# One written order for the RWKV part: the steps of three pairs of heads and of the output projection alternate on TensorE

## The chip, the cores and the metric

The program runs on one core of a Trainium2 chip. What counts is the device time of one execution in microseconds (us). Engines: PE is TensorE (matmuls; PEld is its weight load), DVE is VectorE, ACT is ScalarE, POOL is GpSimd, and SP is SyncE, which issues the DMAs here. Each engine works through its own instructions in the order in which they were emitted, and waits at an instruction until the semaphores it needs have come.

## The reference, cut to what matters

Two transformer blocks run one after the other on 512 tokens of width 1024. The change lies in the second block, in the RWKV mixer (six heads of 64) and in the output projection:

```
w = -softplus(-(w0 + tanh(wd) @ w2)) - 0.5;  a = sigmoid(a0 + ad @ a2);  g = sigmoid(gd) @ g2
kk = k*k_k / max(norm(k*k_k), eps);  k = k*(1 + (a-1)*k_a)
for each token t:  S = S*exp(-exp(w)) + (S @ -kk) (kk*a)^T + v k^T;   y[t] = S r
y = (groupnorm(y)*ln_w + ln_b + sum(r*k*r_k)*v) * g
x = x + concat(attention, y, memory attention) @ w_out
x = x + conv_ffn(rms_norm(x))
```

## The kernel before

Large products are split products: a weight tile is split into a rounded part `wh` (ACT) and a rest `wl` (DVE), and `mm3` issues three matmuls of 128x512, which appear in the profile at lines 161, 163 and 165. A program planner (the tile scheduler) sets the order of the instructions on each engine; what is written first has priority, and a stretch can be given a lower priority.

The token loop is computed in chunks of 64 tokens. The six heads are three pairs (0, 1, 2), one 128-partition tile for each pair; the index `e` is the head in the pair. For a pair there are four parts. `prep` makes decays, normalised keys and transposed copies. `grams` makes the products within the chunks (`NM`) and the first `X` and `XT`. Five levels invert a triangular matrix by doubling: `level` computes per head T = mask*(NM X) (line 1430, evicted by DVE at 1431), then the new X (1435, ACT copy 1437) and the new XT (1440, DVE copy 1442), eight 64x64 matmuls each. `finish` makes `G` (1449), the products `pzx`, `pq`, `py`, a chain of six steps over the chunks (`S`, 1482 and 1483), the group norm, and the split result `obh[i]`, `obl[i]`.

PSUM has eight banks here: two `mm`, two `aux`, three `rw` (levels) and one `wo`.

`w_out_attention`, called W below, is the projection of the five tiles that attention gives: eight blocks (one for each output tile `hl[m]`), each with its own 320 KB load into `wr`, split into `wh` and `wl` (one buffer each), 15 matmuls into the bank `wo`, and an add into `hl[m]` on DVE. It is written with the priority lowered by 3000, and so its blocks fill what the RWKV part leaves. The projection of the RWKV tiles (`w_out`, `w_out_add`) comes last: 512 KB loads straight into three `NM` buffers, tiles 0 and 1 in one accumulation, tile 2 in a second, through the two `mm` banks. The feed-forward part follows.

The parts are called in this order: W (low priority), grams 0, five levels of pair 0, prep 1, grams 1, finish 0, prep 2, levels of pair 1, grams 2, finish 1, levels of pair 2, finish 2, projection. Only the planner mixes them.

Of the kernel before, what the change touches and what calls it, by code (L numbers as in the profile page):

```python
# [10 lines left out]
F32R = mybir.dt.float32r  # L11
# [46 lines left out]
def _build(ctx, tc, ins, out, stop, dbg):  # L58
# [96 lines left out]
    def mm3(pieces, w, xs, first, last, mcol):  # L155

        whi, wlo = w
        xhi, xlo = xs
        c = slice(mcol, mcol + 128)
        for p, s in pieces:  # L160
            pe.matmul(p, whi[:, c], xhi[:, s], start=first, stop=False)  # L161
        for p, s in pieces:
            pe.matmul(p, whi[:, c], xlo[:, s], start=False, stop=False)  # L163
        for p, s in pieces:
            pe.matmul(p, wlo[:, c], xhi[:, s], start=False, stop=last)  # L165
# [669 lines left out]
    RW, WPRI = 3, -3000  # L835
# [361 lines left out]
    def prep(i):  # L1197

        o = B()
        mm = "mm" if i else "aux"  # L1200

# [14 lines left out]
        pe.matmul(pa, lw[32:64, ic], lora[32:64], start=True, stop=True, tile_position=(32, 0))  # L1216
# [3 lines left out]
        dve.tensor_tensor_scan(out=L, data0=reset, data1=sw, initial=0.0, op0=ALU.mult, op1=ALU.add)  # L1220
        pool.tensor_tensor(out=sw, in0=L, in1=sw, op=ALU.subtract)
# [6 lines left out]
        q = work()  # L1228
        act.activation(out=q, in_=k, func=AF.Square, scale=V("k_k", i))
        pc = ps(8, tag="aux")  # L1230
        for b in range(4):
            pe.matmul(pc[:, 2 * b : 2 * b + 2], q[:, b * 128 : (b + 1) * 128], blk2, start=True, stop=True)
        rn = tm(8, "rn", 2)
        act.activation(out=rn, in_=pc, func=AF.Sqrt)
        dve.tensor_scalar(out=rn, in0=rn, scalar1=L2_EPS, scalar2=None, op0=ALU.max)
        dve.reciprocal(out=rn, in_=rn)
        x = q
        dve.tensor_copy(out=x.rearrange("p (c d) -> p c d", d=64), in_=rn.unsqueeze(2).to_broadcast([128, 8, 64]))
        pb = ps(512, tag="aux")
        for b in range(4):  # L1240
            pe.transpose(pb[:, b * 128 : (b + 1) * 128], x[:, b * 128 : (b + 1) * 128], ident)
        kkn = q
        dve.scalar_tensor_tensor(out=kkn, in0=pb, scalar=V("k_k", i), in1=k, op0=ALU.mult, op1=ALU.mult)
# [10 lines left out]
        dve.scalar_tensor_tensor(out=a, in0=a, scalar=V("r_k", i), in1=r, op0=ALU.mult, op1=ALU.mult)  # L1254
        pb = ps(512, tag=mm)
        pe.matmul(pb, blk1, a, start=True, stop=True)
        o.bonus = tp(512, "bonus", "q")
        dve.tensor_tensor(out=o.bonus, in0=pb, in1=v, op=ALU.mult)
        o.RH = RH = tp(1024, "RH").rearrange("p (t e c) -> p t e c", t=4, e=2)
        o.BT, o.KT, o.VT = [tp(512, n, "q") for n in ("BT", "KT", "VT")]  # L1260
        for n, (src, dst) in enumerate(((AR, None), (bt, o.BT), (kt, o.KT), (v, o.VT))):
            pt = ps(512, tag="aux")
            for b in range(4):
                pe.transpose(pt[:, b * 128 : (b + 1) * 128], src[:, b, 0] if dst is None else src[:, b * 128 : (b + 1) * 128], ident)
            if dst is None:
                act.copy(out=RH[:, :, :, 0:64], in_=pt.rearrange("p (t e c) -> p t e c", t=4, e=2))
            else:
                act.copy(out=dst, in_=pt)
        return o

    cur.bufs = {"u": 4, "cv": 4}
    with sub("e_x", "xp"), sub("e_w", "wp"), sub("e_t", "sm"):
# [34 lines left out]
        for n, (name, i) in enumerate(order):  # L1307
# [12 lines left out]
            if name in ("l", "r", "k", "v"):  # L1320
                shifted(u, {"r": 0, "k": 3, "v": 6, "l": 9}[name] + i, lora if name == "l" else rkv[name][i])
                if n == PREPN:
# [3 lines left out]
                    first_prep = prep(0)  # L1326
# [40 lines left out]
    st = [first_prep, None, None]  # L1367
# [22 lines left out]
    def grams(i, o):  # L1390
        o.NM, o.X, o.XT = [], [], []
        for e in range(2):
            hr = hs[e]
            nm = nmt()
            NM = nm.rearrange("p (b m c) -> p b m c", b=4, m=4)
            for b in range(4):
                if b % 2 == 0:
                    p2 = ps(512)
                p = p2[:, b % 2 * 256 : b % 2 * 256 + 256]
                for x, s in ((o.kt, 0), (o.bt, 128)):  # L1400
                    for q in range(2):
# [12 lines left out]
            pt = rw()[:, 0:256]
            for b, r, c in bq:
                pe.matmul(pt[r, c], XT[r, c], ident[r, r], start=True, stop=True)
            act.copy(out=X, in_=pt)
            act.copy(out=o.RH[:, :, e, 64:128], in_=c4(pk))
            o.NM.append(NM)
            o.X.append(X)  # L1420
            o.XT.append(XT)

    def level(o, l):

        for e in range(2):
            X, XT, NM = o.X[e], o.XT[e], o.NM[e]
            T = wk(256, f"T{e}", 2)
            p = rw()[:, 0:256]
            for b, r, c in bq:
                pe.matmul(p[r, c], NM[r, b, 2], X[r, c], start=True, stop=True)  # L1430
            dve.tensor_tensor(out=c4(T), in0=c4(p), in1=lev[l].unsqueeze(1).to_broadcast([128, 4, 64]), op=ALU.mult)
            if l < 4:
                p = rw()[:, 0:256]
                for b, r, c in bq:
                    pe.matmul(p[r, c], XT[r, c], T[r, c], start=True, stop=True)  # L1435
                o.X[e] = wk(256, f"X{e}", 2)
                act.copy(out=o.X[e], in_=p)
            p = rw()[:, 0:256]
            for b, r, c in bq:
                pe.matmul(p[r, c], T[r, c], XT[r, c], start=True, stop=True)  # L1440
            o.XT[e] = wk(256, f"XT{e}", 3)
            dve.tensor_copy(out=o.XT[e], in_=p)

    def finish(i, o):
        G = []
        for e in range(2):
            p = rw()
            for b, r, c in bq:
                pe.matmul(p[r, b * 128 : (b + 1) * 128], o.XT[e][r, c], o.RH[r, b, e], start=True, stop=True)
            g = wk(512, f"G{e}", 1)  # L1450
            act.mul(out=g, in_=p, mul=-1.0)
            G.append(v4(g))
        half = lambda x, q: x.rearrange("p (b q c) -> p b q c", b=4, q=2)[:, :, q]
        pq, pzx = [rw()[:, 0:256] for _ in range(2)], [ps(512), ps(512)]
        for n, (b, r, c) in enumerate(bq):
            for e in range(2):
                pe.matmul(pq[n % 2][hs[e], c], G[e][r, b, 0:64], o.NM[e][r, b, 3], start=True, stop=True)
        for e in range(2):
            hr = hs[e]
            for n in range(8):  # L1460
# [9 lines left out]
        AT = ftmp()  # L1470
        for q in range(2):
            dve.tensor_tensor(out=half(AT, q), in0=pzx[q][:, 0:256].rearrange("p (b c) -> p b c", b=4), in1=eye64.unsqueeze(1).to_broadcast([128, 4, 64]), op=ALU.add)
        lend = o.lend
        S = ftmp()
        XS = ftmp()
        for q in range(2):
            dve.tensor_tensor(out=half(XS, q), in0=pzx[q][:, 256:512].rearrange("p (b c) -> p b c", b=4), in1=lend[:, q::2].unsqueeze(2).to_broadcast([128, 4, 64]), op=ALU.mult)
        act.copy(out=S[:, 64:128], in_=XS[:, 0:64])
        for n in range(1, 7):
            p = ps(64, tag="aux")  # L1480
            for e in range(2):
                pe.matmul(p[hs[e]], AT[hs[e], n * 64 : n * 64 + 64], S[hs[e], n * 64 : n * 64 + 64], start=True, stop=True)
            dve.scalar_tensor_tensor(out=S[:, n * 64 + 64 : n * 64 + 128], in0=p, scalar=lend[:, n : n + 1], in1=XS[:, n * 64 : n * 64 + 64], op0=ALU.mult, op1=ALU.add)
        py = [ps(256) for _ in range(2)]
        for n, (b, r, c) in enumerate(bq):
            for e in range(2):
                pe.matmul(py[n % 2][hs[e], c], G[e][r, b, 64:128], o.NM[e][r, b, 3], start=True, stop=False)
            for e in range(2):
                pe.matmul(py[n % 2][hs[e], c], o.VT[r, b * 128 + 64 * e : b * 128 + 64 * e + 64], o.NM[e][r, b, 1], start=False, stop=True)
        y = ftmp()  # L1490
# [223 lines left out]
```

## Time and profile before

| | us |
|---|---|
| median of 3 runs | 2334.19 (2330.99 to 2338.97) |
| profiled execution, its own time | 2327.18 |
| its span | 2325.4 |
| PE busy in the span | 2230.1 (96%) |
| DVE busy | 1622.7 (70%) |
| ACT busy | 935.1 (40%) |
| mean granted TensorE clock | 0.982 |
| share of PE in the chain that ended last | 87% |

The stretch that the change rewrites begins at 1757 us of the span, when the last attention of the second block is done, and ends at 1948 us, when the last `hl` has been added; the feed-forward part takes the rest. In the windows the clock is a share of full speed: 1.00 is 2.4 GHz, 0.50 is 1.2 GHz. PE's busy time is modelled, and a group of small matmuls that run side by side is best timed from start to start.

### The profile page before, as it was taken

The page shows a single profiled execution, that of the slowest core. Times are in us where ns is not written, and L with a number is a line of the kernel's source. Part 1 is how long each engine was busy: PE and PEld are TensorE (multiplying, and loading weights), DVE is VectorE, ACT ScalarE, POOL GpSimd, SP SyncE. Part 2 cuts the span into 40 slices and gives each one's busy share as a digit, 9 for nine tenths or more (in the row PEclk, how much of TensorE's full clock was granted, in tenths as well). Part 3 has the DMA queues.
Part 4 walks back from the last instruction along what each step waited for, and adds up shares of the span by engine and source line. Part 5 has one row for each costly group of instructions (what it writes and reads, how often), then busy time and mean ns, then how long its engine had stood idle before and what let it go on. Part 6 is the DMA issues. An engine that isn't in the chain of part 4 may idle for free.

```text
span 2325.4 us, 36202 instructions
## 1 busy us (share of the span) xinstructions
PE 2230.1 (96%) x14894; PEld 1843.8 (79%) x14894; DVE 1622.7 (70%) x2625; ACT 935.1 (40%) x1616; POOL 158.0 (7%) x210
## 2 busy tenths in 40 slices
PE   5999899999999999899999999998999979999999
PEld 2777588888888888766689999996777766788887
DVE  4888769877677767776587777677564445866676
ACT  4222543223323334566663443335754323433332
POOL 0000000000000000155400000000241100000000
PEclk8999999999999999999999999999999898999999
DMA  8464423332233311430032222313111003232221
GB/s 320 158 222 158 160 94 133 109 127 91 95 123 109 104 42 74 114 105 28 10 138 98 94 104 76 109 37 108 47 39 35 26 21 118 74 108 91 98 84 55
DMA packets 50817, 228.82 MB, mean 98 GB/s; under 512 B 6331, under 2 KB 10972, under 8 KB 32220
## 3 DMA queue, kind: packets, MB, share of 16 engines
q1 hardware_dynamic: 50652, 226.51, 28.0%
q8 instruction: 117, 1.92, 0.3%
q14 instruction: 48, 0.39, 0.1%
HBM read 213.51 MB, written 6.68 MB: 95 GB/s over the span
## 4 chain that ended last, share of the span: by engine, by line
PE 87%; DVE 5%; ACT 3%; DMA 2%; issue 1%; SPq 0%; POOL 0%; DVEq 0%; ACTq 0%; POOLq 0%
PE mm L161 24%; PE mm L163 24%; PE mm L165 23%; PE po L909 2%; PE aux L905 1%; PE mm L576 1%; DMA raw<-in_ada 1%; PE aux L370 1%; PE sc L887 1%; PE rw L1440 1%; PE mm L783 1%; PE rw L1435 1%; PE sc L888 1%; PE aux L402 1%; PE rw L1430 1%
## 5 line engine op out<-in xcount | busy, mean ns | idle before, releaser
L161 PE MATMUL mm<-xh,wh 128*128 128x512 f32 (+2 forms) x2336 | 658.8, 338 | 13.9 <-ACT xh L479 4.1
L163 PE MATMUL mm<-xl,wh 128*128 128x512 f32 (+2 forms) x2336 | 661.7, 337 | 2.7 <-DVE xl L219 2.1
L165 PE MATMUL mm<-xh,wl 128*128 128x512 f32 (+2 forms) x2336 | 659.4, 337 | 1.6 <-DVE wl L144 1.6
L143 ACT ACTIVATE wh<-raw 128x1024 fp32r<-128x1024 f32 x263 | 274.8, 1057 | 543.6 <-PE mm L163 493.0
L161 PEld LDWEIGHTS mm<-xh,wh 128*128 128x128 f32 x2336 | 410.3, 191 | 68.2 <-issue 6.3
L163 PEld LDWEIGHTS mm<-xl,wh 128*128 128x128 f32 x2336 | 411.6, 190 | 54.3 <-DVE xl L219 3.2
L165 PEld LDWEIGHTS mm<-xh,wl 128*128 128x128 f32 x2336 | 411.1, 190 | 48.9 <-DVE wl L144 2.5
L144 DVE TENSOR_TENSOR wl<-raw,wh 128x1024 fp32r<-128x1024 f32 x263 | 324.6, 1243 | 42.8 <-ACT wh L143 38.3
L161 PE MATMUL mm<-gh,wh 128*128 128x512 f32 (+1 forms) x704 | 253.5, 368 | 2.5 <-ACT gh L288 2.3
L163 PE MATMUL mm<-gl,wh 128*128 128x512 f32 (+1 forms) x704 | 254.0, 366 | 0.1
L165 PE MATMUL mm<-gh,wl 128*128 128x512 f32 x704 | 253.3, 366 | 0.0
L249 DVE TENSOR_TENSOR u<-mm,R 128x256 f32<-128x256 f32 x88 | 37.5, 426 | 179.8 <-PE mm L165 178.1
L161 PEld LDWEIGHTS mm<-gh,wh 128*128 128x128 f32 x704 | 131.1, 188 | 26.8 <-ACT gh L288 3.2
L165 PEld LDWEIGHTS mm<-gh,wl 128*128 128x128 f32 x704 | 130.8, 188 | 23.2
L163 PEld LDWEIGHTS mm<-gl,wh 128*128 128x128 f32 x704 | 130.8, 188 | 23.0 <-DVE gl L289 0.4
L310 DVE SCALAR_TENSOR_TENSOR hl<-mm,mod,hl 128x512 f32<-128x512 f32 x176 | 131.4, 747 | 21.1 <-PE mm L165 20.4
L288 ACT ACTIVATE gh<-cv 128x512 fp32r<-128x512 f32 (+1 forms) x66 | 46.5, 704 | 242.4 <-DVE cv L286 242.4
L271 DVE SCALAR_TENSOR_TENSOR cv<-u,vec,cv 128x512 f32<-128x512 f32 (+1 forms) x132 | 110.3, 837 | 9.9 <-ACT cv L262 9.2
L553 DVE SCALAR_TENSOR_TENSOR accp<-v,dwt,accp 128x798 f32<-128x798 f32 (+2 forms) x118 | 113.9, 975 | 2.6
L272 DVE SCALAR_TENSOR_TENSOR cv<-u,vec,cv 128x512 f32<-128x512 f32 (+1 forms) x132 | 110.7, 840 | 3.1
L284 ACT ACTIVATE cv<-cv 128x512 f32<-128x512 f32 (+1 forms) x66 | 46.4, 704 | 118.2 <-DVE cv L272 118.0
L396 DVE SCALAR_TENSOR_TENSOR ac<-ra,sc,ac 128x512 f32<-128x512 f32 x112 | 81.9, 746 | 1.5 <-DMA ra<-in_ada 1.4
(471 smaller groups left out, 3001.3 us busy)
## 6 DMA issues: line engine op xcount, KB each, us to landing
raw<-in_up SPq DMA_DIRECT2D x63, 1024.0 KB, 4.8
raw<-in_dn SPq DMA_DIRECT2D x33, 1024.0 KB, 4.8
raw<-in_ada SPq DMA_DIRECT2D x24, 1024.0 KB, 6.0
ra<-in_ada SPq DMA_DIRECT2D x48, 512.0 KB, 3.4
raw<-in_pw SPq DMA_DIRECT2D x12, 1024.0 KB, 6.2
S<-vd SPq DMA_DIRECT2D x28, 407.0 KB, 5.4
raw<-in_w_in SPq DMA_DIRECT2D x17, 512.0 KB, 3.3
raw<-in_qkv SPq DMA_DIRECT2D x6, 1024.0 KB, 4.9
```

What stands on the lines that cost most here:

```text
L143: act.activation(out=hi, in_=part, func=AF.Copy)
L144: dve.tensor_tensor(out=lo, in0=part, in1=hi, op=ALU.subtract)
L161: pe.matmul(p, whi[:, c], xhi[:, s], start=first, stop=False)
L163: pe.matmul(p, whi[:, c], xlo[:, s], start=False, stop=False)
L165: pe.matmul(p, wlo[:, c], xhi[:, s], start=False, stop=last)
L271: dve.scalar_tensor_tensor(out=cv[:, 0:CW], in0=u[:, 0:CW], scalar=wv[0], in1=cv[:, 0:CW], op0=ALU.mult, op1=ALU.add)
L272: dve.scalar_tensor_tensor(out=cv[:, 0:CW], in0=u[:, 2 : 2 + CW], scalar=wv[2], in1=cv[:, 0:CW], op0=ALU.mult, op1=ALU.add)
L288: act.activation(out=gh[:, 0:CW], in_=cb[:, 0:CW], func=AF.Copy)
L310: dve.scalar_tensor_tensor(out=hs, in0=p, scalar=g2[i][:, m : m + 1], in1=hs, op0=ALU.mult, op1=ALU.add)
L396: dve.scalar_tensor_tensor(out=a, in0=t[:, q, :], scalar=sc2[:, k, n : n + 1], in1=a, op0=ALU.mult, op1=ALU.add)
L553: dve.scalar_tensor_tensor(out=acc[:, a:b], in0=x, scalar=w, in1=acc[:, a:b], op0=ALU.mult, op1=ALU.add)
L909: pe.matmul(po[64 * e : 64 * e + 64], va[:, t, g], p[:, 256 * e : 256 * e + 256], start=n == 0, stop=n == len(keys) - 1)
```

## The change

`tc.keep_in_program_order` ties matmuls to the order in which they are written. `prep`, `grams`, `levels` (the five levels of a pair, both heads in turn) and `finish` become generators that stop after every step, and a driver calls `go` on them in turn. W becomes a generator of 40 steps of three matmuls, and begins each block with the memory tiles. In `prep` the key norm moves ahead of the decays. In `finish` the gate product moves ahead, and the six chain steps stand between the `py` products. `w_out` loads each RWKV weight in two halves of 256 KB through W's single buffer `wr`, and `w_out_add` adds each of the three tiles by itself, tiles 0 and 1 through the one bank `wo`. The lowered priority is gone.

```diff
-    RW, WPRI = 3, -3000
+    RW = 3
...
+    def levels(o):
+        kept = tc.keep_in_program_order
+        for l in range(5):
+            T = []
+            for e in range(2):
...
+                    kept(pe.matmul(p[r, c], o.NM[e][r, b, 2], o.X[e][r, c], start=True, stop=True))
...
+            yield
...
+    def w_out(n):
+        hi, lo = nmt(F32R), nmt(F32R)
+        for s in (slice(0, 512), slice(512, 1024)):
+            raw = wk(640, "wr")[:, 0:512]
+            sp.dma_start(out=raw, in_=ins["w_ob"][n][:, s])
+            act.activation(out=hi[:, s], in_=raw, func=AF.Copy)
+            dve.tensor_tensor(out=lo[:, s], in0=raw, in1=hi[:, s], op=ALU.subtract)
+        return hi, lo
+    def w_out_add(n, w, tag="wo", kept=tc.keep_in_program_order):
         for m in range(KT):
-            p = ps(512)
-            for i, (hi, lo, x) in enumerate(parts):
-                mm3([(p, slice(0, 512))], (hi, lo), x, i == 0, i == len(parts) - 1, m * 128)
+            p = ps(512, tag=tag)
+            mm3([(p, slice(0, 512))], w, (obh[n], obl[n]), True, True, m * 128, kept)
             dve.tensor_tensor(out=hl[m], in0=p, in1=hl[m], op=ALU.add)
             cur.done[m] = tc.cur_priority
+            yield
-    with tc.high_priority(offset=WPRI):
-        w_out_attention()
-    grams(0, st[0])
...
+    done(grams(0, st[0]))
+    P1, W = prep(1, st[1]), w_out_attention()
+    go(P1)
+    L = levels(st[0])
+    for l in range(10):
+        go(L)
+        go(W)
+        if l in (2, 5, 7, 9):
+            go(P1)
+    G, F0 = grams(1, st[1]), finish(0, st[0])
...
+    w0 = w_out(0)
+    L = levels(st[2])
+    for l in range(10):
+        go(L)
+        go(F1)
+        if l > 2 or l % 2 == 0:
+            go(W)
+    done(F1)
+    w1, w2 = w_out(1), w_out(2)
+    F2 = finish(2, st[2])
+    go(F2)
+    go(W, 2)
+    for _ in range(4):
+        go(F2)
+    done(W)
+    A0, A1 = w_out_add(0, w0), w_out_add(1, w1)
+    for _ in range(5):
+        go(F2)
+        go(A0)
...
+    done(w_out_add(2, w2, "mm", lambda x: x))
```

How instructions move is shown at three places. On PE in the levels of pair 0, before (1435, 1440 and 1430 are new X, new XT and next T of one head; 1232 belongs to prep; the triple is W's, and four more triples follow):

```order
L1435 MATMUL rw<-T_16681,XT_16613 64x64 x8
L1440 MATMUL rw<-XT_16613,T_16681 64x64 x8
L1430 MATMUL rw<-X_16669,NM 64x64 x8
L1232 MATMUL aux<-blk_10505,t 128x2 x4
L161 MATMUL wo<-oh,wh 128x512
L163 MATMUL wo<-ol,wh 128x512
L165 MATMUL wo<-oh,wl 128x512
```

And after (1446 is T, 1455 new X, 1460 new XT):

```order
L1446 MATMUL rw<-X_16444,NM 64x64 x8
L1446 MATMUL rw<-X_16465,NM 64x64 x8
L161 MATMUL wo<-oh,wh 128x512
L163 MATMUL wo<-of,wh 128x512
L165 MATMUL wo<-oh,wl 128x512
L1455 MATMUL rw<-T_16508,XT_16410 64x64 x8
L1460 MATMUL rw<-XT_16410,T_16508 64x64 x8
L1455 MATMUL rw<-T_16519,XT_16433 64x64 x8
L1460 MATMUL rw<-XT_16433,T_16519 64x64 x8
```

Both heads now go through half a level together, and one triple of W stands behind each half instead of a whole block of five.

On ACT between finish 1 and the levels of pair 2, before (1451 is G, 1478 the first chain state, 1545 a split of an RWKV weight, 1437 an X of the first level):

```order
L1451 ACTIVATE G0_17847<-rw_17838 128x512
L1451 ACTIVATE G1_17858<-rw_17849 128x512
L1478 COPY f_17934<-f_17935 128x64
L1545 ACTIVATE NM_18633<-NM_18632 128x1024
L1437 COPY X0_18063<-rw_18054 128x256
```

And after (1590 splits the halves of RWKV weight 0, 1575 is `wh` of W's block 4, 1433 the first X of each head):

```order
L1473 ACTIVATE G0_17665<-rw_17656 128x512
L1473 ACTIVATE G1_17676<-rw_17667 128x512
L1492 COPY f_17777<-f_17778 128x64
L1590 ACTIVATE NM_17873<-wr_17875 128x512
L1590 ACTIVATE NM_17873<-wr_17879 128x512
L1434 COPY RH_17404<-aux_17805 128x4x64
L1575 ACTIVATE wh_17918<-wr_17917 128x640
L1433 COPY X0_17814<-rw_17815 128x256
```

Three splits that read `wr`, each after a load of its own, now stand ahead of the X copy.

On DVE in the last levels of pair 2, before (1431 is T, 1442 XT, 1516 to 1520 the end of finish 1):

```order
L1442 COPY XT1_18173<-rw_18164 128x256
L1516 SCALAR_TENSOR_TENSOR f_17997<-aux_18031,vec_64,f_17997 128x512
L1431 TENSOR_TENSOR T0_18175<-rw_18176,t_16130 128x256
L1517 SCALAR_TENSOR_TENSOR f_17997<-f_17997,vec_64,bonus_17037 128x512
L1518 TENSOR_TENSOR f_17997<-mm_18036,f_17997 128x512
L1520 TENSOR_TENSOR obk1_16385<-f_17997,obr1_16382 128x512
L1442 COPY XT0_18206<-rw_18197 128x256
L1431 TENSOR_TENSOR T1_18208<-rw_18209,t_16130 128x256
```

And after (1576 is `wl` of W's block 5; 1591 with `wr` as its source is the split of a half of RWKV weights 1 and 2; 1448 is T, 1462 XT):

```order
L1576 TENSOR_TENSOR wl_18197<-wr_18195,wh_18196 128x640
L1448 TENSOR_TENSOR T0_18172<-rw_18163,t_16130 128x256
L1448 TENSOR_TENSOR T1_18183<-rw_18174,t_16130 128x256
L1591 TENSOR_TENSOR NM_18312<-wr_18313,NM_18311 128x512
L1550 RECIPROCAL rn_18190<-rn_18190 128x8
L1552 COPY f_18157<-rn_18190 128x512
L1591 TENSOR_TENSOR NM_18312<-wr_18317,NM_18311 128x512
L1462 COPY XT0_18225<-rw_18216 128x256
L1462 COPY XT1_18247<-rw_18238 128x256
L1591 TENSOR_TENSOR NM_18322<-wr_18323,NM_18321 128x512
L1558 TENSOR_TENSOR G0_17665<-aux_18249,G0_17665 128x512
L1559 TENSOR_TENSOR G0_17665<-G0_17665,bonus_16927 128x512
```

After these rows come the last two operations of finish 1's end and T of the next level, then the fourth half (1591), then T of the other head, then a weight of the feed-forward part, and only then XT of the last level. On SP the four half loads stand behind the load of W's block 5 and ahead of that of block 6.

## Rows read from the trace of the kernel before

**Rows 1.** Windows by stretch: length, busy us (PE PEld DVE ACT POOL), clock, DMA.

```profile
1757.00:1822.00 65.00, 64.23 (x1009) 53.14 (x1007) 32.55 (x62) 20.68 (x39) 8.79 (x9) 1.00 0.15 45
1822.00:1868.00 46.00, 38.43 (x657) 30.62 (x653) 25.79 (x50) 20.32 (x35) 7.59 (x7) 0.85 0.04 14
1868.00:1879.00 11.00, 8.68 (x278) 8.37 (x272) 4.20 (x10) 2.87 (x5) 0.00 (x0) 1.00 0.28 98
1879.00:1906.00 27.00, 21.39 (x484) 18.49 (x486) 14.33 (x33) 5.99 (x14) 0.00 (x0) 0.94 0.01 2
1906.00:1948.00 42.00, 37.55 (x363) 26.92 (x357) 20.35 (x38) 9.65 (x18) 0.10 (x1) 0.84 0.01 3
```

**Rows 2.** Timeline of PE: start, us, what (two records for each f32 matmul).

```profile
1758.22 0.50 PE L161 MATMUL wo<-oh,wh 128*128 128x512 f32 x1
...
1761.59 0.39 PE L165 MATMUL wo<-oh,wl 128*128 128x512 f32 x1
...
1763.22 1.12 PE L1216 MATMUL mm<-lora,lw 32*128 32x512 f32 x2
1764.27 0.50 PE L161 MATMUL wo<-oh,wh 128*128 128x512 f32 x1
...
1768.48 0.63 PE L1440 MATMUL rw<-XT,T 64*64 64x64 f32 x16
1768.94 0.63 PE L1430 MATMUL rw<-X,NM 64*64 64x64 f32 x16
...
1813.52 1.92 PE L1449 MATMUL rw<-RH,XT 64*64 64x128 f32 x32
1815.27 0.32 PE L1457 MATMUL rw<-NM,G 64*64 64x64 f32 x4
```

**Rows 3.** Groups of instructions, 1750 to 1950 us: busy us, mean ns, idle before.

```profile
L1431 DVE TENSOR_TENSOR T<-rw,t 128x256 f32<-128x256 f32 x30 | 12.6, 421 | 1.8 <-PE rw L1430 1.3
L1437 ACT COPY X<-rw 128x256 f32<-128x256 f32 x24 | 8.9, 370 | 34.2 <-PE rw L1435 33.9
L1535 DVE TENSOR_TENSOR wl<-wr,wh 128x640 fp32r<-128x640 f32 x8 | 7.1, 886 | 0.7 <-ACT wh L1534 0.7
L1534 ACT ACTIVATE wh<-wr 128x640 fp32r<-128x640 f32 x8 | 5.9, 735 | 17.3 <-PE wo L163 17.3
L1539 DVE TENSOR_TENSOR hl<-wo,hl 128x512 f32<-128x512 f32 x8 | 5.5, 691 | 15.8 <-PE wo L165 15.8
L1214 ACT ACT_TABLE_LOAD x2 | 2.6, 1283 | 1.5 <-PE mm L1212 1.5
L1519 ACT ACTIVATE obr<-f 128x512 fp32r<-128x512 f32 x3 | 1.9, 629 | 9.1 <-DVE f L1518 9.1
```

**Rows 4.** DMA issues of the whole span: count, KB, median us to landing.

```profile
wr<-in_w_oa SPq DMA_DIRECT2D x8, 320.0 KB, 2.9
NM<-in_w_ob SPq DMA_DIRECT2D x3, 512.0 KB, 3.7
t<-in_rwc SPq DMA_DIRECT2D x1, 256.0 KB, 2.6
out<-hl SPq DMA_DIRECT2D x8, 256.0 KB, 2.0
```

**Rows 5.** Windows with a lowered clock, columns as in rows 1.

```profile
1830.00:1840.00 10.00, 9.53 (x85) 5.64 (x84) 4.45 (x9) 7.55 (x9) 1.26 (x1) 0.76 0.00 0
1840.00:1850.00 10.00, 8.58 (x111) 7.88 (x112) 5.64 (x12) 5.11 (x11) 2.55 (x2) 0.56 0.01 2
1880.00:1890.00 10.00, 9.50 (x170) 7.53 (x166) 4.52 (x11) 2.39 (x6) 0.00 (x0) 0.85 0.01 2
1910.00:1920.00 10.00, 7.36 (x153) 5.14 (x148) 3.74 (x11) 0.89 (x3) 0.00 (x0) 0.85 0.01 3
1916.00:1918.00 2.00, 0.88 (x12) 0.55 (x12) 0.97 (x3) 0.65 (x2) 0.00 (x0) 0.76 0.03 8
1920.00:1930.00 10.00, 10.00 (x27) 6.88 (x26) 2.60 (x5) 0.90 (x2) 0.00 (x0) 0.50 0.00 0
```

More of the change, by code (lines that the diff above doesn't have):

```diff
@@ L153, in first_up, with mm3 @@
         return split_w(raw, 0, cur.wa)
-    def mm3(pieces, w, xs, first, last, mcol):
+    def mm3(pieces, w, xs, first, last, mcol, kept=lambda x: x):
         whi, wlo = w
@@ L1227, in prep @@
         act.activation(out=sw, in_=sw, func=AF.Exp, scale=-E05)
[L1228 to L1243, printed above, removed]
+        o.VT = tp(512, "VT", "q")
+        turned(lambda b: v[:, b * 128 : (b + 1) * 128], o.VT)
         o.AR = AR = tp(1024, "AR").rearrange("p (t s c) -> p t s c", t=4, s=2)
@@ L1254, in prep @@
         dve.scalar_tensor_tensor(out=a, in0=a, scalar=V("r_k", i), in1=r, op0=ALU.mult, op1=ALU.mult)
+        yield
+        o.RH = tp(1024, "RH").rearrange("p (t e c) -> p t e c", t=4, e=2)
+        turned(lambda b: AR[:, b, 0], None)
+        yield
+        o.KT, o.BT = [tp(512, n, "q") for n in ("KT", "BT")]
+        turned(lambda b: kt[:, b * 128 : (b + 1) * 128], o.KT)
+        yield
+        turned(lambda b: bt[:, b * 128 : (b + 1) * 128], o.BT)
         pb = ps(512, tag=mm)
-        pe.matmul(pb, blk1, a, start=True, stop=True)
+        kept(pe.matmul(pb, blk1, a, start=True, stop=True))
         o.bonus = tp(512, "bonus", "q")
         dve.tensor_tensor(out=o.bonus, in0=pb, in1=v, op=ALU.mult)
[L1259 to L1269, printed above, removed]
     cur.bufs = {"u": 4, "cv": 4}
@@ L1325, in _build @@
                     sp.dma_start(out=lw, in_=ins["lora2"])
-                    first_prep = prep(0)
+                    first_prep = B()
+                    for _ in prep(0, first_prep):
+                        pass
                     rc = []
@@ L1415, in grams @@
             for b, r, c in bq:
-                pe.matmul(pt[r, c], XT[r, c], ident[r, r], start=True, stop=True)
+                kept(pe.matmul(pt[r, c], o.XT[e][r, c], ident[r, r], start=True, stop=True))
             act.copy(out=X, in_=pt)
-            act.copy(out=o.RH[:, :, e, 64:128], in_=c4(pk))
-            o.NM.append(NM)
+            act.copy(out=o.RH[:, :, e, 64:128], in_=c4(pks[e]))
             o.X.append(X)
[L1421 to L1432, printed above, removed]
+            yield
@@ L1433, in level @@
+    def levels(o):
+        kept = tc.keep_in_program_order
+        for l in range(5):
+            T = []
+            for e in range(2):
                 p = rw()[:, 0:256]
                 for b, r, c in bq:
[L1435 to L1440, printed above, removed]
@@ L1441, in level @@
-            o.XT[e] = wk(256, f"XT{e}", 3)
-            dve.tensor_copy(out=o.XT[e], in_=p)
+                    kept(pe.matmul(p[r, c], o.NM[e][r, b, 2], o.X[e][r, c], start=True, stop=True))
+                T.append(wk(256, f"T{e}", 2))
+                dve.tensor_tensor(out=c4(T[e]), in0=c4(p), in1=lev[l].unsqueeze(1).to_broadcast([128, 4, 64]), op=ALU.mult)
+            yield
+            for e in range(2):
+                X, XT = o.X[e], o.XT[e]
+                if l < 4:
+                    p = rw()[:, 0:256]
+                    for b, r, c in bq:
+                        kept(pe.matmul(p[r, c], XT[r, c], T[e][r, c], start=True, stop=True))
+                    o.X[e] = wk(256, f"X{e}", 2)
+                    act.copy(out=o.X[e], in_=p)
+                p = rw()[:, 0:256]
+                for b, r, c in bq:
+                    kept(pe.matmul(p[r, c], T[e][r, c], XT[r, c], start=True, stop=True))
+                o.XT[e] = wk(256, f"XT{e}", 3)
+                dve.tensor_copy(out=o.XT[e], in_=p)
@@ L1452, in finish @@
             G.append(v4(g))
+        yield
         half = lambda x, q: x.rearrange("p (b q c) -> p b q c", b=4, q=2)[:, :, q]
[L1454 to L1457, printed above, removed]
+        pzx = [ps(512), ps(512)]
         for e in range(2):
@@ L1469, in finish @@
             dve.tensor_tensor(out=half(QT, q), in0=c4(pq[q]), in1=o.AR[:, :, 1, 64 * q : 64 * q + 64], op=ALU.add)
[L1470 to L1483, printed above, removed]
+        yield
         py = [ps(256) for _ in range(2)]
@@ L1562, in _build, with go, done @@
-    st[1] = prep(1)
-    grams(1, st[1])
-    finish(0, st[0])
-    st[2] = prep(2)
-    for l in range(5):
-        level(st[1], l)
-    grams(2, st[2])
-    finish(1, st[1])
-    for l in range(5):
-        level(st[2], l)
-    finish(2, st[2])
-    w_out_add([w_out(n, (obh[n], obl[n])) for n in (0, 1)])
-    w_out_add([w_out(2, (obh[2], obl[2]))])
+            yield
+    def go(g, n=1):
+        for _ in range(n):
+            next(g, None)
+    def done(g):
+        for _ in g:
+            pass
@@ new lines, in _build @@
+    done(grams(0, st[0]))
[8 more added lines that the diff above has]
+    G, F0 = grams(1, st[1]), finish(0, st[0])
+    go(F0)
+    go(W, 2)
+    done(P1)
+    go(F0, 2)
+    go(G)
+    go(F0)
+    P2 = prep(2, st[2])
+    go(P2)
+    go(G)
+    go(F0)
+    go(G)
+    go(F0)
+    go(G)
+    go(F0)
+    done(G)
+    L = levels(st[1])
+    for l in range(10):
+        go(L)
+        go(F0)
+        if l in (1, 3, 5, 7):
+            go(P2)
+        if l > 4 or l % 2 == 0:
+            go(W)
@@ new lines, in _build @@
+    done(F0)
+    done(P2)
+    G, F1 = grams(2, st[2]), finish(1, st[1])
+    go(F1)
+    go(G)
+    go(F1, 2)
+    go(G)
+    go(F1)
+    go(G)
+    go(F1)
+    go(G)
+    go(F1)
+    done(G)
+    w0 = w_out(0)
+    L = levels(st[2])
+    for l in range(10):
+        go(L)
+        go(F1)
+        if l > 2 or l % 2 == 0:
+            go(W)
+    done(F1)
+    w1, w2 = w_out(1), w_out(2)
+    F2 = finish(2, st[2])
+    go(F2)
+    go(W, 2)
+    for _ in range(4):
+        go(F2)
+    done(W)
+    A0, A1 = w_out_add(0, w0), w_out_add(1, w1)
```

153 lines of the change are left out of this document (109 added, 44 removed).

## The prediction

> **What bounds the kernel now.** I read the windows by stretch first, because the change touches 191 of 2325 us and an average over the span says nothing about them. In the first stretch, 1757 to 1822 us, TensorE (PE) is busy 64.23 of 65 us at full clock, and no other engine comes near: there the planner has put nearly all of W in front [rows 1]. In the four stretches behind it PE is busy only 106.05 of 126 us, although DVE, the next engine, is busy 64.67: neither engine is full, so these stretches are bound by the chain PE, eviction, PE within a pair, with nothing left to put into its holes [rows 1]. Then the windows with a lowered clock. Busy time in a window at clock c costs (1 - c) of itself: 0.24 x 9.53 + 0.44 x 8.58 + 0.15 x 9.50 + 0.15 x 7.36 + 0.50 x 10 = 13.6 us [rows 5]. So the kernel before loses about 20 us to idle PE and 14 us to the lower of the clock's two levels: in 1920 to 1930 us the granted share is 0.50, 1.2 GHz, for the whole window, and in the 2 us at 1916 PE had been busy 0.88 us [rows 5]. About 34 us is thus the most that a better order can give.
>
> **Prices.** From start to start: one matmul of W is 3.37 us over 14 steps, 0.24 us, so a triple is 0.72; a plain f32 matmul of 512 columns is 1.05; eight small ones of 64x64 are 0.47, so 0.058 each; G is 1.75 for sixteen of 128 columns, 0.11 each [rows 2]. T takes 0.42 on DVE, the X copy 0.37 on ACT, the splits of W 0.735 (ACT) and 0.886 (DVE), the add into `hl` 0.69 [rows 3]. A W load of 320 KB lands after 2.9 us, 512 KB after 3.7 [rows 4]. The 256 KB half load is new. The nearest row is `t`, the same 256 KB into SBUF from HBM, at 2.6; the store `out`, 2.0, is the low bound and 2.9 the high one, and I take 2.6 [rows 4]. A half split on ACT is 0.63, from the row of the same 512 columns, and its rest on DVE 0.69, from the add of that size [rows 3].
>
> **The change, part by part.** No matmul of size is added or removed; the projection's count is the same (72 products of three tiles, eight outputs, three matmuls each). What is new is where W stands, and two chains of loads through one buffer. I add up PE's work at full clock for five stretches of the new order, cut at the same places of the program as before, and put the waits beside it.
>
> Stretch 1, to pair 1's first T. Of 40 W triples 12 stay: 28 x 0.72 = 20.2 leaves 65 us; the first step of prep 2 comes in (two products of 1.05 and the sums, 3.1). Work 47.9. Waits 6: ACT loads a table for the square root in prep, and three loads of 1.28 now stand ahead of X copies [rows 3]; some seven operations of 0.69 of prep stand ahead of T on DVE, half of them covered by a triple. Bounds 0 and 10. Sum 53.9, before 65.
>
> Stretch 2, the levels of pair 1: 28 groups x 0.47 = 13.2, eight triples 5.8, the rest of finish 0 4.7, the rest of prep 2 3.4 (both counted in small matmuls of 0.058 and full ones of 1.05). A half level's 0.42 or 0.37 lies under the other head's 0.47 to 0.94 and a triple. Only two half levels have no triple, 0.7 us. Sum 27.8, before 46 with 38.43 of PE [rows 1]. This is where the alternation does what it says: 18 us.
>
> Stretch 3, finish 1 with grams 2: G 1.75, grams 32 x 0.11 = 3.5, `pzx` 48 x 0.058 = 2.8, `pq` 0.94, `pk` and `pt` 1.88, two steps of `py` and chain 1.2: 12.1. Here ACT has to pass two half splits and the `wh` of block 4 before the first X of pair 2, and all three are read from the one `wr`. Behind the chain's first state on ACT stand 0.63 + 0.69 (half 1), 2.6 + 0.63 + 0.69 (half 2), 2.9 + 0.735 + 0.37 (block 4 and X), 9.2 us, against some 4.5 of PE work left there: 4.75 us. The two `mm` banks, which grams and `pzx` share, add one turn of 1.75. Wait 6.5. Sum 18.6, before 11.
>
> Stretch 4, the levels of pair 2: 13.2, nine triples 6.5, the rest of finish 1 5.3: 25.0. On SP the four halves of weights 1 and 2 stand between the loads of blocks 5 and 6, and on DVE their rests stand between the XT and T of the last two levels. One turn of `wr` is 2.6 + 0.63 + 0.69 and some 0.1 for the signals: 4.0. From the `wl` of block 5 the fourth half is done after 16.1 us; then T 0.42, a feed-forward split of 1024 columns (0.886 x 1024/640 = 1.4) and two XT copies: G starts 18.9 us after that `wl`. PE has for this time ten groups and parts: new X and XT 1.88, transposes 0.5, T 0.94, XT 0.94, three triples 2.2, 6.4 us together. Wait 12.5. Sum 37.5, before 27. Before, the same weights lay in three `NM` buffers of their own and waited for nobody (512 KB, 3.7, three loads) [rows 4].
>
> Stretch 5, finish 2 and the projection: 12.0, eleven triples 7.9, 72 x 0.24 = 17.3: 37.2. Waits: two switches of W's block with nothing between, 0.735 + 0.886 each, 3.4; sixteen outputs of tiles 0 and 1 through the single bank `wo`, where each next one waits for the add of 0.69 and its signals, 0.85, and some ten have no small step beside them, 8.5; the end of finish 2 ahead of tile 2, 2.1. Sum 51.2, before 42.
>
> Together 53.9 + 27.8 + 18.6 + 37.5 + 51.2 = 189.0, against 191: 2.0 us less at full clock. The 191 hold their 13.6 us of lost clock; the new sum holds none yet. Of the trace, PE fell to 1.2 GHz behind 2 us in which it was busy 0.88 [rows 5]; the new order has two such places, 6.5 idle in 18.6 and 12.5 idle in 37.5 of which 18.9 hold only 6.4 of work, and the start of stretch 5. The longest fall before lasted 10 us whole and its part beside, so one costs about 5 us; I take two, 10 us, between 4 (one short fall) and 16 (three). So the change costs 8 us. The Trainium skill says, in "TensorE: Matmul & The Clock Gate", section "HAM oscillation — how this bites in real kernels", that DMA waits between short bursts of matmuls bring the clock down again and again; rows 5 show such a fall, though behind a chain of evictions, and no row before shows one behind a DMA.
>
> The span lies 1.8 us below its execution's own time of 2327.18, which is 7.0 below the median of 2334.19. The 8 us are a difference of two sums within one execution; I add them to the median: 2342.
>
> **The rivals.** First, the loads are no wait, and the time falls. If a turn of `wr` takes no more than 1.6 us (6.4 of PE work over four turns), the 12.5 of stretch 4, the 4.75 of stretch 3 and the falls behind them, 10, go: 2342 - 27.3 = 2315. For it: DMA is busy 0.01 to 0.28 there, so loads meet no others [rows 1]. Against it: the two splits alone are 1.3 and the shortest landing of this size 2.0 [rows 3, 4]; with 2.0 the turn is 3.4 and the waits only 4 us less. A faster time could also come from smaller waits in stretches 1 and 5, whose 20 us are the softest terms.
>
> Second, no change: the clock stays up, since a triple of W follows nearly each half step. Then 10 us go and the time is 2332. For it: in stretch 1 before, the clock is 1.00 while triples and small steps mix [rows 1]. Against it: in 3 and 4 the waits are too long for the triples that are there. The skill's page "TensorE: Matmul & The Clock Gate", section "Loop structure matters more than you think", holds that copies out of PSUM beside back-to-back matmuls don't disturb the clock; by that rule this rival would win wherever only evictions are waited for.
>
> Third, slower by more: in a fixed order PE can't step over a late eviction. Over the 30 half levels of three pairs, if other operations on ACT or DVE (0.63 to 1.28 us, [rows 3]) stand ahead of T or X more often than I counted, each half level that waits 0.5 beyond its cover adds up to 15 us: 2357. It decides once an operation longer than the triple's 0.72 is ahead in most of them; against it, stretch 2's rows of order show such in a few.
>
> That the order isn't kept is excluded: the rows of the change show the alternation on PE.
>
> **How the numbers follow.** A measurement of this kernel tells about 0.3%, 7.0 us, from no change. Forecast 0.48, 2342 (its turns of 3.4 to 4.3 us and falls of 4 to 16 us spread it from 2333 to 2350; just over half lies above 2341.2); faster through the loads or smaller soft waits 0.22, 2315; clock stays up 0.18, 2332; slower by more 0.12, 2357. Faster by over 0.3% takes the second and a little of the third, 0.25; within 0.3% most of the third and a part of the first, 0.32; slower 0.43. The forecast with its neighbours holds 0.78; to have 8 in 10 the range reaches from 2316, inside the faster case, to 2360. Most of the chance that is not the forecast's is of the other sign, so its own range, 2333 to 2350, is said beside it.
>
> **What the profile after would show.** Right: the levels of pair 1 in about 28 us with hardly an idle stretch; ahead of the first X of pair 2 and the last T and XT an ACT or DVE that waits for `wr` and a DMA; windows at 0.50 right behind these; adds into `hl` alternating with triples at the end, 0.85 apart; the whole from 1757 to the last `hl` near 199 us. Wrong: half loads that land in under 1 us, or ACT idle before X with the weight long there; PE over 95% busy in stretches 3 and 4; a clock of 1.00 throughout; gaps in pair 1's half levels.

## The result and the profile after

The changed kernel takes 2348.62 us (median of five runs, 2347.74 to 2353.70) against 2334.19 before: a ratio of 1.0068, 95% interval 1.0055 to 1.0080. That is 14.4 us slower by the medians and 15.9 by the ratio. The forecast was 2342, slower by 8. Medians and ratios here and below leave out one execution of 11575.4 us, one of the eight of the kernel with the steps of the pairs untied.

Windows of the kernel after, cut as in [rows 1] (the first at the same distance from the last attention, the others at the first T of pair 1, G of finish 1, first T of pair 2, G of finish 2 and the last `hl`); columns as there: length, busy us of PE, PEld, DVE, ACT, POOL, clock, DMA. The last attention comes 3.7 us later than in the profile of before. Before, W began at the first cut; now its first triple starts at 1769.87.

```profile
1760.60:1820.60 60.00, 52.41 (x899) 42.70 (x901) 26.79 (x54) 24.89 (x43) 11.08 (x11) 0.86 0.06 18
1820.60:1852.80 32.20, 30.73 (x582) 23.96 (x573) 20.77 (x43) 10.21 (x21) 1.28 (x1) 1.00 0.03 11
1852.80:1872.70 19.90, 13.65 (x329) 12.87 (x330) 7.76 (x15) 4.40 (x10) 2.90 (x4) 0.86 0.10 32
1872.70:1913.60 40.90, 31.84 (x572) 24.96 (x570) 19.68 (x41) 9.71 (x20) 0.00 (x0) 0.88 0.18 56
1913.60:1968.80 55.20, 43.96 (x399) 29.34 (x398) 28.47 (x51) 11.41 (x20) 0.10 (x1) 0.99 0.15 54
```

| stretch | before | predicted, at full clock | after | of it idle PE | of it lost to the lower clock |
|---|---|---|---|---|---|
| 1 | 65 | 53.9 | 60.0 | 7.6 | 7.3 |
| 2, levels of pair 1 | 46 | 27.8 | 32.2 | 1.5 | 0 |
| 3 | 11 | 18.6 | 19.9 | 6.3 | 1.9 |
| 4, levels of pair 2 | 27 | 37.5 | 40.9 | 9.1 | 3.8 |
| 5 | 42 | 51.2 | 55.2 | 11.2 | 0.4 |
| sum | 191 | 189.0 (+10 clock) | 208.2 | 35.6 | 13.5 |

Idle is length less busy, the clock's loss is (1 - clock) x busy, as in the prediction. Before, the same sums are 20.7 idle and 13.1 lost (13.6 by the windows of [rows 5]). So the 17 us by which these stretches grew are 15 us more of idle PE and 2 us more of busy PE; the clock costs what it cost before. Of the 14.4 us between the medians these stretches are thus more than the whole: the profile of before is an execution 7.0 below its median.

The shape is the forecast one: the levels of pair 1 gain 14 us, and pair 2 and the end give it back, and more.

Stretch 4 is best read in the chain of waits (start, us, what it was), after, from the `wl` of W's block 5 to the last XT:

```profile
1893.73 0.82 DVE wl L1576
...
1894.58 2.63 DMA wr<-in_w_ob
1897.23 0.64 ACT NM L1590
1897.90 0.69 DVE NM L1591
...
1898.62 2.49 DMA wr<-in_w_ob
1901.13 0.64 ACT NM L1590
...
1901.79 0.69 DVE NM L1591
...
1902.51 2.67 DMA wr<-in_w_ob
1905.19 0.64 ACT NM L1590
...
1905.86 0.70 DVE NM L1591
1906.58 2.63 DMA wr<-in_w_ob
1909.23 0.64 ACT NM L1590
...
1909.89 0.62 DVE NM L1591
1910.52 0.41 DVE T L1448
...
1910.97 1.12 PE rw L1460 x16
```

Nothing of PE stands in it for 16 us. Load, split, rest, four times: from one load to the next 4.04, 3.89 and 4.07 us. Of the last level's two T, one stands on DVE behind the third rest and the end of finish 1, the other behind the fourth rest, as the rows of order had shown. PE waits 4.73 us for the first, its longest wait here, and 0.20 for the second.

The queue of ACT in stretch 3, after (start, us, line, and in brackets its idle time and what ended it):

```profile
1860.76 0.62 ACT L1590 ACTIVATE NM<-wr 128x512 fp32r<-128x512 f32 x1
1866.35 0.63 ACT L1590 ACTIVATE NM<-wr 128x512 fp32r<-128x512 f32 x1 [4.96 <-DMA wr<-in_w_ob]
1866.88 0.35 ACT L1434 COPY RH<-aux 128x256 f32<-128x256 f32 x1
1870.61 0.74 ACT L1575 ACTIVATE wh<-wr 128x640 fp32r<-128x640 f32 x1 [3.37 <-DMA wr<-in_w_oa]
1871.25 0.35 ACT L1433 COPY X<-rw 128x256 f32<-128x256 f32 x1
```

PE is done with the first X of pair 2 by 1865, but ACT copies it at 1871.25, behind two loads that have not landed (4.96 and 3.37 us). PE itself waits here for two other operations that stand behind the same splits: 2.2 us for RH on ACT, behind the second half, and 2.7 us for a chain state on DVE, behind the `wl` of W's block 4.

The clock, after, in the four places where it was lowered:

```profile
1762.00:1771.00 9.00, 7.88 (x63) 5.83 (x63) 2.67 (x6) 6.07 (x9) 1.90 (x3) 0.50 0.01 5
1812.00:1819.00 7.00, 5.91 (x98) 5.51 (x100) 2.89 (x4) 4.36 (x8) 4.00 (x4) 0.54 0.01 4
1868.00:1877.00 9.00, 6.31 (x101) 5.26 (x101) 2.80 (x8) 1.54 (x4) 0.00 (x0) 0.50 0.26 75
1908.00:1914.00 6.00, 4.15 (x39) 3.09 (x41) 3.94 (x7) 2.22 (x3) 0.00 (x0) 0.52 0.52 175
```

The last two follow the two waits for `wr`. The first follows the start, where grams 0 waits for its own evictions and no triple of W is there to fill:

```profile
1758.50 0.45 PE L1427 MATMUL aux<-q,NM 64*64 64x64 f32 x8 [0.53 <-DVE NM L1417]
1761.14 0.50 PE L1427 MATMUL aux<-q,NM 64*64 64x64 f32 x8 [2.19 <-DVE NM L1417]
1763.12 1.12 PE L1432 MATMUL rw<-ident,XT 64*64 64x64 f32 x16 [1.48 <-POOL XT L1421]
```

At the end, PE's waits from 1913 to 1969 us (line, released by: us, times, longest), and two neighbouring outputs of tile 0:

```profile
PE wo L161 <- DVE hl L1599: 7.6, 12, 1.0
PE wo L161 <- DVE hl L1581: 2.0, 3, 0.9
```

```profile
1932.71 0.50 PE L161 MATMUL wo<-obr,NM 128*128 128x512 f32 x1 [0.26 <-DVE hl L1581]
1933.59 0.36 PE L1506 MATMUL mm<-NM,G 64*64 64x64 f32 x8
1934.44 0.50 PE L161 MATMUL wo<-obr,NM 128*128 128x512 f32 x1 [0.26 <-DVE hl L1599]
```

They start 1.73 us apart although a step of finish 2 lies between: `wo` is free only after the add.

### The profile page after: what moved, and what is told of

The parts are those of the page before. It is cut to its first block, busy times and chain, and to the rows that moved or that the text cites. A ratio compares the mean times of both kernels' runs of the same rounds, so it can differ in the third digit from the quotient of the medians.

```text
span 2346.8 us, 36204 instructions
## 1 busy us (share of the span) xinstructions
PE 2236.5 (95%) x14894; PEld 1841.7 (78%) x14894; DVE 1630.8 (69%) x2639; ACT 937.4 (40%) x1622; POOL 157.2 (7%) x210
## 4 chain that ended last, share of the span: by engine, by line
PE 86%; DVE 6%; DMA 3%; ACT 3%; issue 1%; POOL 1%; SPq 0%; DVEq 0%; ACTq 0%; POOLq 0%
PE mm L161 23%; PE mm L163 23%; PE mm L165 23%; PE po L909 1%; PE aux L905 1%; PE mm L576 1%; PE wo L161 1%; DMA raw<-in_ada 1%; PE aux L370 1%; PE sc L887 1%; PE mm L783 1%; DMA wr<-in_w_ob 1%; PE sc L888 1%; PE aux L402 1%; DMA vd<-v 1%
```

## The experiments

Each kernel is the changed one with one edit unless said otherwise. Each was timed beside the kernel before on its chip, so the ratios are to be compared; the last column is the difference of ratios to the changed kernel times 2334 us, good to some 4 us. So a difference of 3.5 or 3.7 is by itself not clear of noise.

| kernel | median | ratio to before | against the changed kernel |
|---|---|---|---|
| changed | 2348.62 | 1.0068 (1.0055 to 1.0080) | |
| own buffers for the halves | 2335.64 | 1.0012 (1.0003 to 1.0021) | -13.1 |
| halves of weights 1, 2 written late | 2345.49 | 1.0052 (1.0039 to 1.0065) | -3.7 |
| one add for tiles 0 and 1 | 2345.85 | 1.0053 (1.0039 to 1.0067) | -3.5 |
| wo and rw banks in turn | 2342.41 | 1.0035 (1.0023 to 1.0047) | -7.7 |
| W begun inside grams 0 | 2341.99 | 1.0034 (1.0020 to 1.0047) | -7.9 |
| own buffers + one add + W early | 2331.47 | 0.9994 (0.9985 to 1.0003) | -17.3 |
| no ties | 2333.58 | 1.0002 (0.9993 to 1.0010) | -15.4 |
| triples untied | 2338.34 | 1.0023 (1.0013 to 1.0033) | -10.5 |
| steps of the pairs untied | 2342.32 | 1.0038 (1.0025 to 1.0051) | -7.0 |
| no ties + own buffers | 2320.59 | 0.9945 (0.9931 to 0.9960) | -28.7 |
| W early, one add, two banks, six buffers | 2323.01 | 0.9950 (0.9936 to 0.9964) | -27.5 |
| the same without ties | 2324.38 | 0.9956 (0.9942 to 0.9970) | -26.1 |

**Own buffers for the halves.**

```diff
-            raw = wk(640, "wr")[:, 0:512]
+            raw = wk(512, "wq", 4)
```

> Changed kernel, but the halves of the RWKV weights have four 512-column buffers of their own; W's blocks keep wr to themselves. If the turns of the one wr are what stretches 3 and 4 wait for: in the changed kernel's trace 12.5 us of idle PE between the wl of block 5 and G, 4.9 us ahead of pair 2's first T, and 3.5 and 2.6 us of lowered clock behind them, 23 us together; some of it comes back as the splits still stand in the queues, so 2326 to 2333 us against 2348.6. If the levels' own chain would have taken that time anyway: above 2343.

13.1 us less, a little under the 16 expected at least, and not the second case. Stretch 4 in this kernel (columns as above):

```profile
1872.72:1901.97 29.25, 28.09 (x574) 22.30 (x570) 17.94 (x39) 7.42 (x16) 0.00 (x0) 0.99 0.10 32
```

From 40.9 to 29.3 us, 1.2 idle, clock 0.99: the turns of `wr` are what stretch 4 waited for. Stretch 3 fell by 1.8 us only, not by 4.9 and its clock, since with buffers free the planner put all six splits there, and the last two wait for their load:

```profile
1868.76 1.24 ACT L1590 ACTIVATE NM<-wq 128x512 fp32r<-128x512 f32 x2 [3.96 <-DMA wq<-in_w_ob]
1869.91 0.35 ACT L1434 COPY RH<-aux 128x256 f32<-128x256 f32 x1
```

**The same halves, later.**

```diff
-    w1, w2 = w_out(1), w_out(2)
     F2 = finish(2, st[2])
...
     done(W)
+    w1, w2 = w_out(1), w_out(2)
     A0, A1 = w_out_add(0, w0), w_out_add(1, w1)
```

> Changed kernel, but the halves of RWKV weights 1 and 2 are written behind the end of W; the one buffer wr stays. If it is their place ahead of the last levels' copies that costs, and not the number of buffers: the 12 us of idle PE of stretch 4 and 2.6 us of lowered clock go, the four turns of 4 us lie beside the eight triples of tile 0 at the end (1.75 us apart, 14 us), 2336 us. If the turns only move and hold up the triples of tile 1: above 2344.

Stretch 4 shrinks just as much, to 29.3 us, but only 3.7 us of it reach the end, which is within the noise: the second case by its number. In the profiled execution (2352.06 us, the slowest of its five) stretch 5 takes 68.1 us instead of 55.2:

```profile
1900.00:1922.00 22.00, 19.07 (x293) 14.58 (x289) 8.66 (x18) 4.62 (x8) 0.00 (x0) 1.00 0.09 28
1922.00:1964.00 42.00, 33.95 (x149) 20.00 (x143) 19.91 (x34) 5.26 (x10) 0.00 (x0) 0.55 0.10 32
```

PE waited 1.69 us at 1922 for the add of W's last block and then ran the whole projection at the lower level. The add was late because the rest of the first moved half stood ahead of it on DVE and waited for its load and split (start, us, line, idle time and what ended it):

```profile
1921.88 0.63 ACT L1590 ACTIVATE NM<-wr 128x512 fp32r<-128x512 f32 x1 [4.40 <-DMA wr<-in_w_ob]
1922.54 0.69 DVE L1591 TENSOR_TENSOR NM<-wr,NM 128x512 fp32r<-128x512 f32 x1 [4.19 <-ACT NM L1590]
1923.15 0.68 DVE L1581 TENSOR_TENSOR hl<-wo,hl 128x512 f32<-128x512 f32 x1
```

So a turn of `wr` held up one triple here too, and in this execution the lower clock behind it cost more than stretch 4 had gained. The mean clocks of the other four executions, 0.976 to 0.980, lie close to those of the changed kernel, 0.977 to 0.982; how much the clock takes in them isn't shown.

**The bank at the end.** One add for two tiles, as before the change, and then two banks with an add for each:

```diff
+    def w_out_two(w0, w1):
...
+            mm3([(p, slice(0, 512))], w0, (obh[0], obl[0]), True, False, m * 128, kept)
+            yield
+            mm3([(p, slice(0, 512))], w1, (obh[1], obl[1]), False, True, m * 128, kept)
+            dve.tensor_tensor(out=hl[m], in0=p, in1=hl[m], op=ALU.add)
...
-    A0, A1 = w_out_add(0, w0), w_out_add(1, w1)
+    A0 = A1 = w_out_two(w0, w1)
```

> Changed kernel, but tiles 0 and 1 of the projection accumulate in one bank and are added once, in the same places, as in the kernel before. If the turn of the one bank wo sets the pace at the end: triples of different outputs stand 1.75 us apart there, of which 0.72 is work, so eight turns of 1.03 fewer, 8.2 us, 2340 us. If the end of finish 2 sets the pace there: no more than 3 us, 2346 or above.

```diff
-            p = ps(512, tag=tag)
+            p = ps(512, tag=tag if n == 2 or m % 2 == 0 else "rw")
```

> Changed kernel, but the sixteen outputs of tiles 0 and 1 go in turn through wo and one of the three rw banks, each tile still added by itself. If the turn of the one bank paces the end: the 7.6 us that PE waits there for additions go, 2341 us. If finish 2's own chain paces it, which the smaller gain with one addition for two tiles speaks for (3.5 of 8.2 us): 2346 or above.

One add saves 3.5 us, in the trace 2.7 of stretch 5: with half the adds PE still waits six times, 4.1 us, because the written order puts two triples behind one another at a bank that is not free. Two banks save 7.7 us, bring stretch 5 from 55.2 to 46.8, and PE no longer waits at `wo` for an add of tiles 0 and 1 (7.6 us in the changed kernel):

```profile
1915.46:1962.29 46.83, 41.64 (x399) 29.25 (x398) 28.08 (x51) 11.44 (x20) 0.10 (x1) 0.99 0.18 64
```

So it is the bank's turn and not finish 2. The rival of the second expectation falls.

**W begun inside grams 0.**

```diff
-    done(grams(0, st[0]))
-    P1, W = prep(1, st[1]), w_out_attention()
+    W = w_out_attention()
+    G = grams(0, st[0])
+    for _ in range(4):
+        go(G)
+        go(W)
+    done(G)
+    P1 = prep(1, st[1])
     go(P1)
```

> Changed kernel, but W begins inside grams 0: five of its triples stand between the products of grams 0 and ahead of the first T, and so five fewer at the end. If the start without filling is what costs there: 4.2 us of idle PE (0.53 + 2.19 + 1.48) and 4.3 us of lowered clock behind it go, 2340 us. If the triples are only taken from a place that needs them as much: within 3 us of 2348.6.

7.9 us less, near the number expected, but not by the mechanism (the edit puts four triples there, not five). From the last attention to the first T it takes 15.2 us, as without the edit (15.4): idle falls from 4.2 to 1.7 and the clock's loss from 3.1 to 2.2, and the triples done there fill that. The gain shows in stretches 3 and 4, 17.5 and 35.4 us instead of 19.9 and 40.9: W's blocks stand earlier, so no load of W lies ahead of pair 2's first X on ACT, and only three of the four halves are split ahead of G.

**The three together.**

> The three edits together: own buffers for the halves, one addition for tiles 0 and 1, W begun inside grams 0. If the three costs are separate: 2348.6 - 18 - 8 - 8 = 2314 us, under the kernel before (2334). If they share the same slack (the end waits for finish 2, whatever comes earlier): 2325 or above.

17.3 us, against a sum of 24.5 for the three by themselves. The number is that of the second case, but not its reason, for stretch 5 shrinks to 45.5 us, so finish 2 does not hold the end. The likelier reason, not shown, is that own buffers remove the turns which the early start also shortened; and a sum of three such differences is itself uncertain by some 7 us (an estimate from the intervals).

**No ties.** `keep_in_program_order` replaced by nothing wherever it stands, the calls as they are:

```diff
-    kept = tc.keep_in_program_order
+    kept = lambda x: x
```

> Changed kernel with the calls in the same alternating sequence, but no matmul tied to the order in which it is written: the planner may let one pass another. If the fixed order itself costs (PE stands at a late step while another is ready): 2340 us or less. If the loss sits in the queues of ACT and DVE and in wr, which this leaves as they are: 2345 to 2352.

The first case, and more of it than expected: 15.4 us, as much as the whole slowdown of 15.9. By the timeline of PE, 20 of W's 40 triples now lie ahead of G of finish 0 (changed kernel: 10; before: all 40), none in finish 2 (changed: 11), and stretch 5 takes 38.0 us. They also run in blocks of five again (start, us, two records for an f32 matmul):

```profile
1879.25 0.50 PE L161 MATMUL wo<-oh,wh 128*128 128x512 f32 x1
...
1882.92 1.03 PE L1536 MATMUL rw<-f 64*64 64x64 f32 x28
```

3.67 us for fifteen matmuls. `wr` still costs: stretch 4 has 20 triples in it and 8.9 us idle, at a clock of 0.81.

**Which ties.** The triples alone untied, and the steps of the pairs alone:

> Changed kernel, but the triples of W and of the projection are not tied to the written order; prep, grams, levels and finish stay tied. If the 14 us that the untied order gained come from triples that may pass a waiting step of a pair: 2336 us or less. If they come from steps of a pair passing each other: 2345 or above.

> Changed kernel, but prep, grams, levels and finish are not tied to the written order; the triples of W and of the projection stay tied among themselves. If the steps of a pair passing each other is what gains: 2336 us or less. If the triples are: 2345 or above. A triple may then be passed by a step too, so that both ties off one by one may each give the whole: then either tie alone does no harm.

10.5 and 7.0 us: each does part, and both at once do 15.4. That the triples do more than the steps isn't clear of noise. Neither expectation's clean case holds.

**No ties and own buffers.**

> No ties, and four own buffers for the halves: the fourth corner beside the changed kernel (2348.6), own buffers alone (2335.6) and no ties alone (2333.6). If the tied order only hurts where wr makes it wait: 2333, no more than either edit alone. If both costs are separate: 13 + 15 us, 2320.

28.7 us, against 13.1 + 15.4 = 28.5: within noise the two costs add up, the second case. All of W is now done before the levels of pair 1, since none of its loads stands behind a half in `wr`; stretch 4 takes 24.4 us, and four triples of tile 0 already lie in it. It is 0.55% faster than the kernel before.

**The order mended by hand, with and without ties.**

> W begun inside grams 0, one addition for tiles 0 and 1 with wo and rw banks in turn, and six own buffers for the halves, so that every half is loaded long before its split. If the costs found so far add up: from 2331 with the three edits, 4 us of waits for additions and 2 us of waits for a load go, 2325 us, under the kernel before. If finish 2's chain is the bound at the end: 2330.

> The fastest kernel so far (2323.0: W begun early, one addition for tiles 0 and 1 through wo and rw, six own buffers) without ties. If the written order is worth something once nothing in it waits for a load or a bank: slower than with it, 2328 or above. If the ties are a cost by themselves: 2315 or below.

0.9950 and 0.9956, intervals that overlap. With ties, 2323.01, the first case of its expectation holds; without, 2324.38 lies between the two cases. Once W begins early, two banks take the outputs of one add, and each half has its buffer, the ties neither cost nor gain anything that is measured here, although without them all of W runs before the levels of pair 1 again. So the alternation isn't slow by itself; it was tied around waits. All these kernels share the new order inside `prep` and `finish`; no run puts the old one back, so what that part costs or gains stays open.

## Why the prediction was right, and where its steps were not

The direction and the waits that it named were right; the size was about half: 8 us forecast, 14.4 by the medians. For the five stretches the sum said 199 us with the clock's falls; they took 208.2. At full clock PE's work came to 159.1 us (172.6 busy less 13.5 for the clock), where the sum had 149.3. The waits came to 35.6, where it had 39.7, and the clock's loss to 13.5, where it had 10.

*Right.* Stretch 4: turn of `wr` 4.0 (measured 3.9 to 4.1, landing 2.5 to 2.7) and 18.9 us from that `wl` to G (1894.55 to 1913.60, 19.05). Own buffers took 11.7 us out of this stretch, the clock's part included. The wait itself was 9.1 and not 12.5, for PE was busy 10.0 us of that time and not 6.4. Stretch 3: 18.6 (19.9), with 4.75 of wait for `wr` (4.9) and 1.75 for the turn of the `mm` banks (1.4). But the wait comes at that place whatever load the planner puts there, as own buffers showed. Stretch 5: 8.5 for the sixteen outputs at the one bank (7.6), shown by the two banks. One term there did not come as described: for the switches of W's block the sum had 3.4 (two of them are 3.24) for splits, and PE waited 2.0, for adds at the same bank.

*Mis-sized: the work, 9.8 us short.* The triple is part of it. 0.72 came from W in one dense row [rows 2]. Between small steps a triple costs more, after:

```profile
1883.61 0.50 PE L161 MATMUL wo<-oh,wh 128*128 128x512 f32 x1
...
1884.50 1.15 PE L1446 MATMUL rw<-X,NM 64*64 64x64 f32 x32
1885.58 1.12 PE L1530 MATMUL mm<-lora,lw 64*128 64x512 f32 x2
```

That is 0.89 from its start to the next step's, and both T take 1.08 instead of 0.94. The 56 triples of W and of tiles 0 and 1 stand in 39 groups with other steps between them. At 0.17 for each group that is 6.6 us that the sum lacked (an estimate: what a triple costs in each of these places was not read). In stretch 2, where PE idles 1.5 us only, eight triples and five pairs of T explain 2.1 of the 3.6 us by which 30.7 us are busy and not 27.1. Of the rest no run shows the cause.

*The clock: size about right (13.5 for 10), places half wrong.* Two falls behind the loads were foreseen. The two others, at the start and behind the table loads of prep 2 (PE waits 1.21 us there for ACT at line 1234), are in stretch 1, which was predicted without any. And as the kernel before loses as much, the clock is no reason for the difference. At full clock the forecast was from 177.4 to 189.0 us, and it became 177.9 to 194.7. The falls at 1868 and 1908 came behind waits for loads, by way of ACT and DVE. The Trainium skill, in "TensorE: Matmul & The Clock Gate", section "HAM oscillation — how this bites in real kernels", says that waits for a DMA between short bursts of matmuls bring the clock down again and again; these two falls agree. In stretch 2 PE waits for evictions alone, 1.5 us in all, and the clock is 1.00. The Trainium skill, in "TensorE: Matmul & The Clock Gate", section "Loop structure matters more than you think", says that copies out of PSUM beside back-to-back matmuls don't disturb the clock; stretch 2 agrees. The fall at 1762 shows the other side: ahead of it PE had waited 0.53 and 2.19 us for evictions, and for no load.

*Weighed only as a rival: what the tie costs.* The sum took the written order as given. The third rival, PE that can't step over a late operation, priced only the half levels of the pairs (15 us in all). The untied kernel is 15.4 us faster, but that the two numbers agree is luck, for the time lay elsewhere: the half levels of pair 1 wait hardly at all, and the start, the loads and the bank at the end are where tied triples stood behind a wait or came too late. There is luck in the nearness of the forecast as well. In the stretches the sum is 9.2 us short, and only because its errors partly cancel: the work 9.8 too small, the clock's loss 3.5 too small, the waits 4.1 too large. Between the medians the miss is 6.6 us. The range, 2316 to 2360, held faster times as well as slower ones.

*The rivals.* No wait at the loads: fallen, the turn is 4.0 us. Clock stays up: fallen, there are four falls. Slower by more, 2357, because of the half levels: fallen in pair 1, where PE idles 1.5 us. What the runs leave open is how the 15.4 us of the ties divide among start, triples and bank, since the three edits by hand overlap with each other and with `wr`.

## What to carry to other kernels

Before a filler is tied into a written order, ask for each of its steps what it waits for. A single buffer's turn (load, split, rest: 4 us here) and a single bank's turn (1.75 us for 0.9 of work) then become waits of the whole engine, and no busy share shows it beforehand. The planner's order on the other engines is part of the change too: a split that waits for its load holds up whatever stands behind it, so give such loads buffers of their own, or tie nothing. And price a step by a row in which it stands between the same neighbours as it will, not by a dense run of itself.

## What was not expected of the hardware

At the lower level of the clock a sparse stretch can stay there. The triples of tiles 0 and 1, with gaps at each bank turn, run in the changed kernel at full clock, 22.17 of 30 us busy:

```profile
1931.00:1961.00 30.00, 22.17 (x164) 13.22 (x164) 17.13 (x30) 2.86 (x6) 0.00 (x0) 1.00 0.05 18
```

and with the halves written late the same triples, 2.43 us apart, run for 42 us at 0.55. The difference that the trace shows is the 2 us ahead, in which PE was busy 0.31 us:

```profile
1922.00:1924.00 2.00, 0.31 (x11) 0.17 (x5) 1.46 (x3) 0.51 (x1) 0.00 (x0) 1.00 0.00 0
1924.00:1926.00 2.00, 1.88 (x24) 1.28 (x25) 0.98 (x3) 0.19 (x1) 0.00 (x0) 0.78 0.39 131
1926.00:1928.00 2.00, 2.00 (x23) 1.23 (x22) 1.36 (x2) 0.47 (x2) 0.00 (x0) 0.50 0.00 0
```

It is one execution, and its kernel's slowest, so that the wait brought the clock down and kept it there is a reading and not shown.
